# Two-layer FoX and NSA decoder on one core: the second layer's attention units reordered, its filling work spread, and its first output tiles begun apart

## The chip, the cores and the metric

The kernel runs on one core of a Trainium2 chip. The metric is device time in microseconds (us) of one execution. Three timed runs of the kernel before gave a median of 1553.28 us (1551.80 to 1553.96).

A core has five engines that run side by side, each in its own fixed order: TensorE (PE, matrix products and transposes), VectorE (DVE), ScalarE (ACT), GpSimd (POOL), and SyncE (SP), from whose queue this kernel issues all its DMA transfers. An engine waits at the head of its queue until what that instruction needs is there; everything behind it waits too. PEld is PE's loading of the stationary operand, which overlaps with its products.

## The reference, cut to what matters

```python
def reference(x, norm_g, fox..., nsa..., final_g):        # x: 1024 tokens x 1024, f32
    for i in range(2):
        h = rmsnorm(x, norm_g[i])
        y = fox_mixer(h, ...) if i % 2 == 0 else nsa_mixer(h, ...)
        x = x + y
    return rmsnorm(x, final_g)

def nsa_mixer(h, ...):                    # 16 heads of 64, 4 groups of 4 heads share k and v
    q, kc, vc, ks, vs, kw, vw, gate, z = split(h @ w_in)
    o_c = attention over 63 compressed blocks             # before the stage of this case
    o_s = softmax(q ks^T, only 8 chosen blocks of 64 keys) vs       # branch 0, "chosen"
    o_w = softmax(q kw^T, only the last 512 keys) vw                # branch 1, "window"
    o = g0 * o_c + g1 * o_s + g2 * o_w
    return (o * silu(z)) @ w_out
```

The change touches the stage that computes `o_s` and `o_w` for all heads, the projection `z` that is computed beside it, and the last product with `w_out`, the residual and the final norm. All matrix products are made of three products of split operands (a high part and a remainder), which keeps float32 accuracy.

## The kernel before, in words

**Layer 0** (FoX attention) and the projections and the compressed branch of layer 1 take the first 982 us and stay as they are.

**Layer 1's attention** (L1351) works on "supers": one head `h` and one half `s` of the tokens (s=1: tokens 512 to 1023, s=0: 0 to 511), in the order s=1, s=0 for each head, 32 in all. A super has eight *units* (`unit`, L1235), one for each branch `y` and each query tile `qi` of 128 tokens. A unit has: the score product on PE into a PSUM tile of two banks from `psS1`, of which there are two (L1256); on DVE the mask and the row minimum, from PSUM to the SBUF tile `P_n` (L1263); on ACT the exponential (L1266). A chosen unit (y=0) leaves `P_n` in a buffer of its own. A window unit (y=1) uses one of four `Pw` buffers, and POOL makes two half-width copies in `hl_n` from it (L1269 and L1270, three buffers), which a DMA transposes into `hT_n` (L1272). Then the *steps* (L1313) of the super follow: transposes of the chosen scores on PE (L1288), their split copies on ACT and DVE (`split_t`, L150 and L151), and the products with v for both branches on PE (L1296 to L1298); transposes of the first blocks need all four chosen units of the super. `finish` (L1323) scales the sums (`u_n` on DVE, `ot_n` on POOL), and after every second head `close` (L1336) transposes, multiplies with silu(z) (L1347) and writes to `oF` in DRAM (L1348).

The units of the next super are laid between the steps of the one before (`run_attn`, L180). In `units` (L1279) the order is: s=1 first the four chosen, then the four window units; s=0 first window, then chosen. Over the supers this gives eight window units in a row, then eight chosen ones.

**The filler** (L1184) is other work that is laid between the main work by `merge` (L208): both sides yield costs (written by hand, in ns of PE work), and the filler goes on while its sum is under 0.33 times that of the main side. It consists of the silu(z) projections of layer 1, two heads at a time (`nsa_zs`, L1167, with 24 products of 512 columns for each half, a yield of 650 behind each three), and of `load_wout` (L521), which loads `w_out` from DRAM in two halves and splits it: four DMAs, then eight copies on ACT (L530) and eight subtractions on DVE (L531) with a yield of 200 after every two. W_out goes into the memory of `hT`, so a half can only be loaded after the last projection of that half of the tokens. The projection of pair p waits until pair p-2 is done, since `z` has four buffers; pairs 6 and 7 are done half by half together.

**The output** (`out_layer`, L673, called for layer 1 at L1361): for each of eight tiles of 128 tokens, in the order 4, 5, 6, 7, 0, 1, 2, 3, the columns of `oF` are loaded (`of`, L692, a buffer of the pool `wp` that is open during the whole program), split by ACT and DVE (L693, L694), and multiplied with W_out in 48 products of 512 columns (L133 to L135) into two PSUM banks; then residual, norm and store. Tile 4 is done in two steps, of rows 0 to 3 and 4 to 7 of the eight blocks of 128 rows (block p belongs to heads 2p and 2p+1).

**What sets the order.** Each engine's order is planned before the run: the order of the program text is the priority, and an instruction is placed earlier where its engine would be free and its data and buffers are there. Pools are opened and released in the text; the pool `fo` of the output (gB, the residual tiles `xr`, the norm tiles) is opened after the pool `at` of the attention is released, and takes its memory:

```python
at.release()
kv[0].release()
fo = tc.alloc_tile_pool(name="fo", bufs=1, reuse_waits="tile")
```

## Time and profile before

| | |
|---|---|
| median of three timed runs | 1553.28 us |
| the profiled execution, its time | 1553.53 us |
| its span (first to last instruction) | 1551.7 us |
| layer 1's attention, from its first scores to its last sums | about 982 to 1453 us |
| output of layer 1, to the end | about 1453 to 1552 us |
| PE busy, share of the span | 1434.4 us, 92% |
| DVE busy | 1063.7 us, 69% |
| ACT busy | 803.3 us, 52% |
| POOL busy | 556.5 us, 36% |

A row of the page or of a view names the engine, the line of the kernel and the operation with its tiles (out<-in). A group's row gives the count, the busy time, the mean duration in ns, and the idle time of the engine just before it with what ended that. A row of the waits gives the engine and line that waited, what it waited for, the sum in us, the number of waits and the longest. "SPq" rows are the issue of DMAs. A busy PE is not PE at its peak, as products are pipelined and their ends are modelled.

### The profile page before, as it was taken

To read this page: it belongs to the slowest core of one execution; us is meant where nothing else is said; L and a number is where in the kernel's file an instruction comes from. 1 tells how busy PE (TensorE), PEld (TensorE's weight loads), DVE (VectorE), ACT (ScalarE), POOL (GpSimd) and SP (SyncE) were. 2 spreads that over 40 slices of the span, in tenths; PEclk is the share of its full clock that TensorE was granted. 3 is DMA by queue.
4 is the path that set the end of the run, shared out by engine and by line. 5 is a ranking of instruction groups with operands and counts; after the bars stand their busy time and mean duration, and the time that the engine had idled before them with its cause. 6 is when DMAs were issued, how large, how long until landed. Compare 5 with 4: busy or idle time off the path is not lost.

```text
span 1551.7 us, 29460 instructions
## 1 busy us (share of the span) xinstructions
PE 1434.4 (92%) x10488; PEld 1188.4 (77%) x10488; DVE 1063.7 (69%) x2756; ACT 803.3 (52%) x2025; POOL 556.5 (36%) x604
## 2 busy tenths in 40 slices
PE   5999999999999787999999979899898998888898
PEld 4888888888787666878888768687787877667686
DVE  6586878778787755457364687787686777678433
ACT  5364646545555643233133655566565666567321
POOL 1232323222233500043241342557647657345300
PEclk9999999999999889999999999999999999899899
DMA  7796767867878756343345586757756856674642
GB/s 263 223 183 146 163 155 156 172 160 149 178 156 174 166 104 231 95 133 96 126 134 176 149 202 179 206 123 151 168 122 143 195 118 137 151 167 113 161 138 95
DMA packets 405763, 242.72 MB, mean 156 GB/s; under 512 B 332464, under 2 KB 353840, under 8 KB 405360
## 3 DMA queue, kind: packets, MB, share of 16 engines
q1 hardware_dynamic: 405616, 240.84, 63.5%
q8 instruction: 83, 1.36, 0.4%
q14 instruction: 64, 0.52, 0.1%
HBM read 120.96 MB, written 44.11 MB: 106 GB/s over the span
## 4 chain that ended last, share of the span: by engine, by line
PE 61%; DVE 16%; ACT 6%; DMA 6%; POOL 6%; issue 4%; SPq 1%; POOLq 0%; DVEq 0%; ACTq 0%
PE S_n L1256 4%; DVE P_n L1263 3%; PE y L133 3%; PE y L135 3%; PE y L134 3%; POOL hl_n L1270 3%; PE ptp_n L1288 2%; PE v L133 2%; PE v L135 2%; PE v L134 2%; PE S L579 2%; PE S L580 2%; PE q L133 2%; PE O L613 2%; PE k L133 2%
## 5 line engine op out<-in xcount | busy, mean ns | idle before, releaser
L1266 ACT ACTIVATE P_n<-P_n,m_n 128x640 f32<-128x640 f32 (+7 forms) x256 | 187.0, 731 | 74.6 <-DVE m_n L1265 37.3
L1256 PE MATMUL S_n<-nk,nq 128*128 128x320 f32 (+5 forms) x768 | 189.0, 356 | 19.4 <-DVE m_n L1263 18.6
L597 ACT ACTIVATE P<-P,m 128x512 f32<-128x512 f32 (+1 forms) x192 | 116.9, 610 | 133.2 <-DVE m L588 132.3
L568 POOL TENSOR_TENSOR Bd<-B,tri 128x128 f32<-128x128 f32 x128 | 62.3, 501 | 245.3 <-DVE m L588 228.5
L1263 DVE CUSTOM_DVE_ANT_0 P_n<-S_n,wmask 128x128 f32<-128x128 f32 (+1 forms) x192 | 113.5, 598 | 53.4 <-POOL hl_n L1270 37.7
L1256 PEld LDWEIGHTS S_n<-nk,nq 128*128 128x128 f32 x768 | 125.2, 194 | 32.3 <-DVE m_n L1263 23.3
L1270 POOL TENSOR_TENSOR hl_n<-P_n,hl_n 128x640 f16<-128x640 f32 (+4 forms) x128 | 141.5, 1109 | 7.5
L599 DVE SCALAR_TENSOR_TENSOR hl<-P,hl 128x512 f16<-128x512 f32 (+1 forms) x192 | 124.1, 664 | 21.8 <-ACT hl L598 20.7
L150 ACT ACTIVATE pth_n<-ptp_n 128x512 f16<-128x512 f32 (+1 forms) x160 | 86.6, 546 | 76.1 <-PE ptp_n L1288 75.4
L1288 PE MATMUL ptp_n<-ident,P_n 128*128 128x128 f32 x576 | 98.2, 292 | 19.3 <-DVE ptl_n L151 10.3
L151 DVE SCALAR_TENSOR_TENSOR ptl_n<-ptp_n,pth_n 128x512 f16<-128x512 f32 (+1 forms) x160 | 100.5, 634 | 20.8 <-ACT pth_n L150 20.1
L1269 POOL CAST hl_n<-P_n 128x640 f16<-128x640 f32 (+4 forms) x128 | 74.1, 584 | 98.7 <-ACT P_n L1266 78.4
L133 PE MATMUL y<-wo,ohi 128*128 128x512 f32 x240 | 96.8, 403 | 8.0 <-ACT ohi L693 8.0
L1288 PEld LDWEIGHTS ptp_n<-ident,P_n 128*128 128x128 f32 x576 | 71.3, 149 | 33.1 <-DVE ptl_n L151 11.9
L134 PE MATMUL y<-wo,ohi 128*128 128x512 f32 x240 | 96.0, 400 | 0.0
L135 PE MATMUL y<-wo,olo 128*128 128x512 f32 x240 | 94.9, 398 | 0.9 <-DVE olo L694 0.9
L598 ACT ACTIVATE hl<-P 128x512 f16<-128x512 f32 (+1 forms) x192 | 92.5, 513 | 4.3 <-DMA pT<-hl 2.8
L1296 PE MATMUL O_n<-nv,pth_n 128*128 128x64 f16 x576 | 76.1, 199 | 3.7 <-ACT pth_n L150 3.7
L579 PE MATMUL S<-KH,Q 128*128 128x512 f32 (+1 forms) x192 | 68.8, 372 | 10.6 <-DVE m L588 10.4
L1297 PE MATMUL O_n<-nv,pth_n 128*128 128x64 f16 x576 | 74.9, 197 | 0.0
L1298 PE MATMUL O_n<-nv,ptl_n 128*128 128x64 f16 x576 | 72.2, 197 | 0.0
L1296 PEld LDWEIGHTS <-pth_n 128*128 128x128 f16 x576 | 53.8, 101 | 21.4 <-ACT pth_n L150 9.1
(384 smaller groups left out, 4517.0 us busy)
## 6 DMA issues: line engine op xcount, KB each, us to landing
nq<-qD SPq DMA_DIRECT2D x64, 256.0 KB
B<-cD SPq DMA_DIRECT2D x16, 512.0 KB
wo<-wD SPq DMA_DIRECT2D x16, 512.0 KB
nq<-qD SPq DMA_DIRECT2D x64, 128.0 KB
of<-oF SPq DMA_DIRECT2D x12, 512.0 KB
x<-in_x_dram SPq DMA_DIRECT2D x8, 512.0 KB
wst_k<-in_fox_w_dram SPq DMA_DIRECT2D x8, 512.0 KB
wst_v<-in_fox_w_dram SPq DMA_DIRECT2D x8, 512.0 KB
```

Of the source, the lines that this page charges most:

```text
L133: T.matmul(ps, wh, mh, start=first, stop=False, **kw)
L134: T.matmul(ps, wh, ml, start=False, stop=False, **kw)
L135: T.matmul(ps, wl, mh, start=False, stop=last, **kw)
L151: V.scalar_tensor_tensor(lo[:, 0:n], pt[:, 0:n], scale, h, OP.mult, OP.subtract)
L597: A.activation(L[:, 0:n], L[:, 0:n], AF.Exp, bias=init, scale=-1.0, accum_out=self.lr[:, col + c:col + c + 1])
L599: V.scalar_tensor_tensor(lo[:, cs], L[:, 0:n], UP, hi[:, cs], OP.mult, OP.subtract)
L1256: T.matmul(ps[:, b, 0:w], self.q[x][:, qi * P:(qi + 1) * P], k[:, k0 + b * w:k0 + b * w + w], start=(x == 0), stop=(x == 1))
L1263: V.tensor_tensor_reduce(dst, src, mk, 1.0, 3e38, OP.add, OP.min, m)
L1266: A.activation(L, L, AF.Exp, bias=m, scale=-1.0, accum_out=self.l[:, y, qi:qi + 1])
L1270: G.tensor_tensor(hl[:, n:2 * n], L, hl[:, 0:n], OP.subtract)
L1288: T.transpose(pt[:, (x + i) * P:(x + i + 1) * P], L[:, kb * P - k0:(kb + 1) * P - k0], ident)
L1296: T.matmul(o, hi, v[:, 0:64], start=first, stop=False)
```

## The change

Seven edits, all but the last in layer 1's attention and its filler, in the order of the diff:

1. `merge` gets `cap`: a filler that was held up may be behind its share by at most `cap` (1400 in the call for layer 1), and what is beyond that is forgotten.
2. `load_wout` yields 2000 after the four DMAs of a half, and 400 before each copy, for layer 1 alone.
3. `nsa_zs`: pair 6 is projected like the pairs before it; only pair 7 is done half by half, each followed by a half of W_out.
4. There are five `Pw` buffers in place of four, and one `u` buffer in place of two.
5. `units` alternates for both halves: qi 0 chosen, qi 0 window, qi 1 chosen, and so on.
6. The filler's share is 0.36 in place of 0.33.
7. `out_layer` takes `early`, for layer 1 tiles 4 and 5. Their products with blocks 0 to 3 and 4 to 6 are written ahead of the loop of tiles, into the two double banks of the scores; block 7 follows in the loop. For all tiles of layer 1, `of` comes from the pool `fo` with three buffers in place of `wp` with one, and the residual is loaded after the products are issued.

```diff
-    def merge(main, fill, ratio, off=0.0, until=None, rebase=False):
+    def merge(main, fill, ratio, off=0.0, until=None, rebase=False, cap=1e9):
...
             paid += c
+            base = min(base, done + cap - ratio * (paid + off))
             while done < base + ratio * (paid + off):
...
             dma(f(lo[:, k, :]), wD[i][r * P:(r + 1) * P, :])
+        if i:
+            yield 2000
         for k in range(4):
             for c in range(2):
+                if i:
+                    yield 400
                 cs = slice(c * 512, c * 512 + 512)
...
-    def out_layer(ow, w, src, res, g, after, name):
+    def out_layer(ow, w, src, res, g, after, name, early=()):
+
         gB = ow.tile([P, D], F32, name=f"gB{name}")
...
+        def tiles(t):
+            if not early:
+                return out_tiles(f"{name}_{t}")
+            of = ow.tile([P, KC, P], F32, tag="of", bufs=3, name=f"of{name}_{t}")
+            return of, *out_parts(f"{name}_{t}")
+
+        def products(t, tile, ys, ks):
+            of, oh, ol = tile
+            c = slice(ks[0], ks[-1] + 1)
+            dma(of[:, c, :], src[:, t * P:(t + 1) * P].rearrange("(k p) t -> p k t", p=P)[:, c, :])
+            A.copy(oh[:, c, :], of[:, c, :])
+            V.tensor_tensor(ol[:, c, :], of[:, c, :], f(oh[:, c, :]), OP.subtract)
+            for half, ts in enumerate(cs):
+                if len(ys) <= half:
+                    ys.append(ps_a(f"y{name}_{t}_{half}"))
+                for k in ks:
+                    wh, wl = w[k // 4]
+                    mm3(ys[half], oh[:, k, :], ol[:, k, :], wh[:, k % 4, ts], wl[:, k % 4, ts], k == 0, k == KC - 1)
+
+        begun = {}
+        for t in early:
+            ps = ps_s2(f"y{name}_{t}")
+            begun[t] = tiles(t), [ps[:, half, :] for half in range(2)]
+            for ks in (range(0, 4), range(4, 7)):
+                products(t, *begun[t], ks)
         for t in (4, 5, 6, 7, 0, 1, 2, 3):
...
+            if t in begun:
+                tile, ys = begun.pop(t)
+                steps = (range(7, 8),)
+            elif not ys:
+                tile = tiles(t)
             for ks in steps:
...
+                products(t, tile, ys, ks)
+            dma(xt, res[tk, :])
...
     def nsa_zs():
-        for p in range(6):
+        for p in range(7):
             wo_copy(1, p)
             if p >= 2:
                 yield lambda p=p: ("done", p - 2) in ready
             yield from nsa_z(p, next_w(("z", p)))
-        for p in (6, 7):
-            wo_copy(1, p)
-        yield lambda: ("done", 4) in ready
-        ws = [next_w(("z", 6)), next_w(("z", 7))]
+        wo_copy(1, 7)
+        yield lambda: ("done", 5) in ready
+        w = next_w(("z", 7))
         for half in (1, 0):
-            for p in (6, 7):
-                yield from nsa_z(p, ws[p - 6], (half,))
-                if half == 1:
-                    yield lambda: ("done", 5) in ready
+            yield from nsa_z(7, w, (half,))
             yield from load_wout(h1, 1, half)
...
-                L = at.tile([P, 640], F32, tag="Pw", bufs=4, name=f"P_{nm}")[:, 0:n]
+                L = at.tile([P, 640], F32, tag="Pw", bufs=5, name=f"P_{nm}")[:, 0:n]
...
-            return [self.unit(y, qi) for y in ((0, 1) if self.s else (1, 0)) for qi in range(4)]
+            return [self.unit(y, qi) for qi in range(4) for y in range(2)]
...
-            u = at.tile([P, 4, 2, 64], F32, tag="u", bufs=2, name=f"u_{self.name}")
+            u = at.tile([P, 4, 2, 64], F32, tag="u", bufs=1, name=f"u_{self.name}")
...
-    merge(run_attn([NsaSuper(h, s) for h in range(H) for s in (1, 0)], 0.8, 3), filler, 0.33)
+    merge(run_attn([NsaSuper(h, s) for h in range(H) for s in (1, 0)], 0.8, 3), filler, 0.36, cap=1400)
...
-    out_layer(fo, ready["wout"], oF, x1, a["final_g"], after1, 1)
+    out_layer(fo, ready["wout"], oF, x1, a["final_g"], after1, 1, (4, 5))
```

## The prediction, made before the result was known

> **What bounds the kernel now.** I read the page first, then busy time by stretches, then the waits of layer 1's attention, and last the order of single instructions at its two odd places. By stretches (us of PE, PEld, DVE, ACT, POOL busy; then PE's granted clock, DMA share, GB/s):

> ```profile
> 982.00:1453.00 471.00, 422.46 (x4932) 359.41 (x4931) 347.48 (x949) 295.40 (x706) 274.95 (x320) 0.95 0.66 146
> ...
> 1110.00:1120.00 10.00, 7.04 (x59) 6.45 (x60) 5.37 (x15) 3.47 (x9) 7.92 (x11) 0.66 0.68 136
> 1340.00:1350.00 10.00, 3.53 (x36) 2.84 (x34) 3.89 (x7) 4.60 (x9) 0.00 (x0) 0.71 0.71 234
> 1380.00:1390.00 10.00, 5.65 (x94) 4.15 (x91) 4.88 (x16) 4.47 (x12) 5.71 (x9) 0.93 0.98 201
> 1400.00:1453.00 53.00, 46.27 (x611) 39.44 (x610) 38.77 (x113) 33.07 (x82) 32.20 (x39) 0.87 0.53 116
> 1453.00:1552.00 99.00, 88.75 (x384) 72.09 (x382) 34.89 (x58) 22.50 (x49) 2.52 (x3) 0.97 0.42 136
> 300.00:400.00 100.00, 99.65 (x637) 81.42 (x636) 81.99 (x242) 56.27 (x144) 26.37 (x32) 1.00 0.72 155
> ```

> In the 471 us of attention no engine is full: PE stands idle for 471 - 422.5 = 48.5 us, DVE is busy for 347.5/471 = 74%, and layer 0's attention (last row) shows that DVE can reach 82%. Engines wait for each other in turn. Who waits for whom between 980 and 1480 us (sum, times, longest):

> ```profile
> POOL hl_n L1269 <- ACT P_n L1266: 78.4, 18, 16.1
> ACT pth_n L150 <- PE ptp_n L1288: 75.4, 64, 5.0
> ...
> DVE P_n L1263 <- POOL hl_n L1270: 37.7, 36, 3.3
> ...
> PE S_n L1256 <- DVE m_n L1263: 18.6, 18, 2.6
> ...
> ACT wo L530 <- DMA wo<-wD: 11.7, 4, 4.9
> ```

> The first and the third row belong together: POOL starves for up to 16.1 us at a stretch, and at other times DVE stands still for POOL, 36 times, with all that is queued behind it (the split copies `ptl_n`, for which PE's products wait). That is the order of eight window and eight chosen units. Where it is worst (1110 to 1120 us) PE's idle time also brings its clock down to 0.66.

> [...]

> **The change, part by part.** *Alternating units, fifth `Pw` buffer.* Costs of the units' instructions (first count, busy us, mean ns, idle before; then count, shortest/median/longest ns, first and last start):

> ```profile
> L1263 DVE CUSTOM_DVE_ANT_0 P_n<-S_n,wmask 128x128 f32<-128x128 f32 (+1 forms) x192 | 113.5, 598 | 53.4 <-POOL hl_n L1270 37.7
> L1270 POOL TENSOR_TENSOR hl_n<-P_n,hl_n 128x640 f16<-128x640 f32 (+4 forms) x128 | 141.5, 1109 | 7.5
> L1269 POOL CAST hl_n<-P_n 128x640 f16<-128x640 f32 (+4 forms) x128 | 74.1, 584 | 98.7 <-ACT P_n L1266 78.4
> ...
> L1263 DVE CUSTOM_DVE_ANT_0 P_n<-S_n,bias 128x1024 f32<-128x1024 f32 x16 | 19.5, 1220 | 0.3 <-PE S_n L1256 0.2
> L1266 ACT ACTIVATE P_n<-P_n,m_n 128x1024 f32<-128x1024 f32 x16 | 18.3, 1147 | 0.4 <-DVE m_n L1263 0.3
> ...
> L1270 POOL TENSOR_TENSOR hl_n<-P_n,hl_n x128: 425/1314/1919, 996.5 to 1445.7; 128x640 f16<-128x640 f32 x64, 128x128 f16<-128x128 f32 x16, 128x256 f16<-128x256 f32 x16, 128x384 f16<-128x384 f32 x16
> ...
> L1331 DVE TENSOR_TENSOR u_n<-O_n,l_n x32: 677/685/693, 1010.1 to 1452.7; 128x512 f32<-128x512 f32 x32
> ...
> L1263 DVE CUSTOM_DVE_ANT_0 P_n<-S_n,wmask x192: 280/618/826, 992.3 to 1446.2; 128x640 f32<-128x640 f32 x64, 128x128 f32<-128x128 f32 x32, 128x256 f32<-128x256 f32 x32, 128x384 f32<-128x384 f32 x32
> ```

> POOL needs (141.5 + 74.1)/16 = 13.5 us for a head's eight window units, all in one run; in the other half of the head it has next to nothing. Over the whole head POOL has 275/16 = 17.2 us of work and DVE 347.5/16 = 21.7, against a mean period of 471/16 = 29.4. Alternating gives POOL one window unit (1.7 us on average) for every two units of DVE, so neither waits long. The amount removed lies between nothing (the wait moves elsewhere) and the whole 37.7 us. PE's idle time that it can be taken from is 48.5 less the W_out stalls below, some 37. I take half of that, **-18**, since DVE in-order waits are partly covered by filler on PE. A stage of 471 - 31 = 440 us (all parts) has DVE at 79%, below layer 0's 82%, so DVE would not forbid it. One `u` buffer instead of two costs nothing: `u_n` comes once in (1452.7 - 1010.1)/31 = 14.3 us, and POOL reads it at once when it isn't backed up.

> [...]

> *W_out's copies.* ACT and DVE had them queued ahead of the attention's own work before the data was there:

> ```profile
> 1343.72 1.14 ACT L530 CAST wo<-wo 128x512 fp32r<-128x512 f32 x2 [4.88 <-DMA wo<-wD]
> ...
> L530 ACT CAST wo<-wo x16: 607/617/618, 1343.7 to 1396.0; 128x512 fp32r<-128x512 f32 x16
> ...
> 1341.28 7.25 DMA wo<-wD
> ```

> Two stretches of 10 us lost 6.5 and 4.4 us of PE there. The 2000 behind the DMAs are 2000/0.36 = 5.6 us of main work, which at the stage's pace (by the yields in the code a head has 17 us of it: 7.1 of scores, 9.5 of steps, 0.4 of closing; it takes 29) is more than 7.25 us. So the wait of 11.7 us falls; between 0 and 11.7, I take **-10**. The 16 copies (0.62 us ACT, 0.69 DVE each) stay. As the waits of 6.0 us per half count as filler, pair 7 and W_out need (2 x 5.2 + 2 x 6.0)/0.36 = 62 us of main work behind head 11; four heads have about 68, so W_out just ends with the last head.

> *Pair 6, cap and 0.36.* Before, pairs 6 and 7 came in a block at 1326 to 1341 us, and the last stretch (1400 to 1453) had no filler at all: PE idle 6.7 us. Spread out, it fills some of that: 0 to -6.7, I take **-3**.

> *The first output tiles.* Here I expect a loss. Issue of DMAs on SP at the end of both layers, and tile 4's copies on ACT:

> ```profile
> 559.47 14.11 SPq L600 DMA_TRANSPOSE pT<-hl  x6
> 584.88 0.33 SPq L638 DMA_DIRECT2D oF<-z  x1
> 586.93 0.36 SPq L692 DMA_DIRECT2D of<-oF  x1
> 590.56 0.33 SPq L638 DMA_DIRECT2D oF<-z  x1
> 591.00 0.38 SPq L675 DMA_DIRECT2D gB<-in_norm_g_dram  x1
> ...
> L692 SPq DMA_DIRECT2D of<-oF x9: 370/377/381, 1265.9 to 1514.7; - x9
> ...
> 1453.53 0.33 SPq L1348 DMA_DIRECT2D oF<-no  x1
> 1455.54 0.38 SPq L692 DMA_DIRECT2D of<-oF  x1
> 1457.14 0.32 SPq L1348 DMA_DIRECT2D oF<-no  x1
> 1457.55 0.38 SPq L675 DMA_DIRECT2D gB<-in_final_g_dram  x1
> 1457.99 0.44 SPq L696 DMA_DIRECT2D xr<-x  x1
> ...
> 1458.35 0.62 ACT L693 CAST ohi<-of 128x512 fp32r<-128x512 f32 x1 [7.34 <-DMA of<-oF]
> ```

> gB needs only an input, yet in both layers it is issued 0.4 us behind the attention's last write to `oF`; in layer 0 SP had nothing to do between 573.6 and 584.9 and did not issue it. I read this as: a pool that takes over a released pool's memory opens, in the planned order, only behind the last user of the old one. `of` from `wp`, which is always open, was issued at 1265.9, and tile 4's first 24 products were run beside the last head (from 1449.3). The change moves `of` into `fo`: then it comes behind the last write and behind gB, and no early product is early. Before, the pieces on the path were:

> ```profile
> 1449.31 0.31 PE y L133
> ...
> 1457.99 5.95 DMA xr<-x
> 1464.03 0.70 DVE xr L704
> ...
> 1467.23 0.80 PE y L133
> ...
> 1544.96 0.24 PE y L135
> ```

> From 1467.23 to 1545.20 PE ran 336 products without a stop, 0.232 us each. After, with the last write again at 1457.14: `of` is issued where xr was, at 1457.99, and lands after 2.8 us (the 256 KB from 1455.54 to 1458.35, alone) to 5.95 us (xr, behind gB). I take 4.4, between the two as it is half of xr's size: 1462.4, ACT's copy 0.62, PE starts at 1463.0, and has all 384 products to do: 89.1 us, and 0.7 for tile 6, whose operands wait for tile 4's buffers: 1552.8 against 1545.2, **+7.6** (6.0 to 9.2). Residuals now loaded after the products no longer hold ACT, which is why it isn't 11.

> The sum: -18 - 10 - 3 + 7.6 = -23.4. The profiled execution took 1553.5 us (1.8 around its span), 0.25 over the median, so this goes for the median too: **1530 us**; with each part at its ends but alternating at 8 to 30, 1515 to 1545.

> **The rivals.** *The early tiles are early.* If `of` opens with the last use of the tiles it lies on (masks, last read until 1446.8), 60 more products fit into PE's time up to 1467.2. Of those 20.4 us PE used 11.1 for 48 products and an estimated 3.7 for the last head (by the yields 2.8 of steps and 0.9 of closes), so 5 are free: -5 in place of +7.6, **1517**. For it: `of` of tile 4 did get hoisted before. Against: gB in both layers.

> *Alternating wins nothing*: the wait moves from DVE to PE's transposes, the stage is DVE's. Then -10 - 3 + 7.6: **1548**. For it: heads 14 and 15 have no filler and are no quicker than others; against: POOL's gaps of 16 us.

> *Alternating costs.* For s=1 the last chosen score moves from fourth to seventh place of eight, and the transposes of the next steps need it: DVE 1.22 + 0.08, ACT 1.15 + 0.19 = 2.64 us. Before, four window units of 0.82 us on DVE lay between; now one, so 1.8 us are open per head, 16 x 1.8 = 29: 1530 + 29 = **1559**. It decides from 23.4/16 = 1.5 us a head. Against: for s=0 it is the other way round (before, nothing lay between), and PE has the next super's scores and filler to run meanwhile.

> **How the numbers follow.** Forecast 0.60, early tiles early 0.13, nothing won 0.14, alternating costs 0.13. The range 1508 to 1556 leaves out most of the costly case and the lower part of the early one, about 0.2. A change under 0.2%, 3.1 us, can't be told from none: faster than 1550.2 are nearly all of the forecast and the early case and two thirds of "nothing won", 0.80; same 0.07; slower 0.13.

> **What would show it.** Right: DVE's wait for POOL (L1270) below 15 us; ACT's wait for W_out's DMA below 3; POOL's longest starvation below 6 us; first `y` product only behind the last `O_n` product, its `of` issued behind gB. Wrong: `of` issued before the last `oF` write (first rival); PE's transposes or scores waiting for ACT's `P_n` or DVE's `m_n` (18.6 us now) longer by more than DVE's wait for POOL falls (third); or first to last `u_n`, 442.6 us now, not under 430 (second).

## The result, and the profile after

The changed kernel takes **1529.26 us** (median of 4 runs, 1522.62 to 1530.55) against 1552.54 us before (median of 4, 1549.75 to 1553.96). The ratio is 0.9843, with a 95% interval of 0.9816 to 0.9870. The forecast was 1530. Executions of one kernel differ by some us, and the longer ones mostly had the lower mean granted clock (the kernel before on one chip: 1549.70 us at 0.972, 1559.88 at 0.963). The profiled execution took 1529.59 us with a span of 1527.8, which is 23.9 us less than the span before.

The total hides two sums of opposite sign. The last write to `oF` is issued at 1422.07 in place of 1457.14, so the attention ends 35.1 us earlier. From there to the end of the span it was 94.6 us and is now 105.7, so the output takes 11.2 us more. Lines are those of the changed kernel: the scores are L1275, the mask and minimum L1282, the window units' copies on POOL L1288 and L1289, the last sums `u_n` L1350, the write to `oF` L1367, W_out's copies L536 and L537, `of` L696, its copies L697 and L698.

Busy time of the changed kernel by stretches (PE, PEld, DVE, ACT, POOL, then PE's granted clock, DMA share, GB/s): the attention, and the start of the output.

```profile
982.00:1418.00 436.00, 406.90 (x4936) 348.66 (x4934) 352.74 (x957) 296.29 (x706) 284.54 (x322) 0.98 0.73 160
1425.00:1430.00 5.00, 0.83 (x2) 0.61 (x3) 0.85 (x2) 1.13 (x2) 0.00 (x0) 0.50 1.10 294
1430.00:1435.00 5.00, 5.00 (x15) 4.01 (x15) 1.97 (x5) 1.63 (x4) 0.00 (x0) 0.62 1.10 339
```

The first row answers to the 471 us row of before. PE's idle time is 436 - 406.9 = 29.1 us in place of 48.5, and PE's busy time for as many products is 406.9 in place of 422.46, which fits the clock, granted at 0.98 in place of 0.95 (worked out below for the order alone). DVE is now busy for 81%.

The waits of the changed kernel between 980 and 1480 us (sum, times, longest), those of the prediction's list:

```profile
POOL hl_n L1288 <- ACT P_n L1285: 107.8, 58, 6.3
...
PE S_n L1275 <- DVE m_n L1282: 8.3, 13, 1.4
...
ACT wo L536 <- DMA wo<-wD: 7.2, 4, 2.6
DVE P_n L1282 <- POOL hl_n L1289: 6.8, 7, 1.1
```

DVE's wait for POOL fell from 37.7 to 6.8 us. POOL still starves, for more in sum than before, but for 6.3 us at the longest in place of 16.1, in 58 short pieces. ACT's wait for W_out's data fell only from 11.7 to 7.2. PE's wait for the scores' buffers, which DVE frees, fell from 18.6 to 8.3.

SP's issue of DMAs at the end of the changed kernel, and then the chain of waits there (start, duration):

```profile
1422.07 0.33 SPq L1367 DMA_DIRECT2D oF<-no  x1
1422.48 0.38 SPq L682 DMA_DIRECT2D gB<-in_final_g_dram  x1
1422.92 2.96 SPq L696 DMA_DIRECT2D of<-oF  x5
```

```profile
1422.92 5.56 DMA of<-oF
1428.50 0.63 ACT ohi L697
1429.17 0.80 PE y L133
1429.97 0.43 PE y L134
```

gB comes 0.4 us behind the last write to `oF`, and `of` right behind gB: no tile is early. The last `O_n` product ended at 1417.15 and the first `y` product starts at 1429.17. The first products take 0.43 us each in place of 0.23, at a clock of 0.50 to 0.62 (the rows from 1425 to 1435 above); the full clock is back after 1433.8. The clock was already halved at 1416.72, behind a stop of PE of 2.3 us in the last head, and stayed so through two more stops of 1.6 and 9.3 us.

### The profile page after: what moved, and what is told of

Read it like the earlier page. It is cut to its first block, busy times and chain, and to the rows that moved or that the text cites. A ratio compares the mean times of both kernels' runs of the same rounds, so it can differ in the third digit from the quotient of the medians.

```text
span 1527.8 us, 29541 instructions
## 1 busy us (share of the span) xinstructions
PE 1421.9 (93%) x10488; PEld 1179.8 (77%) x10488; DVE 1066.2 (70%) x2759; ACT 805.1 (53%) x2028; POOL 565.1 (37%) x604
## 4 chain that ended last, share of the span: by engine, by line
PE 63%; DVE 16%; ACT 8%; DMA 6%; issue 4%; POOL 1%; SPq 1%; POOLq 0%; DVEq 0%; ACTq 0%
PE S_n L1275 5%; PE y L133 3%; PE y L135 3%; PE y L134 3%; PE ptp_n L1307 3%; ACT P_n L1285 2%; DVE P_n L1282 2%; PE v L133 2%; PE v L135 2%; PE v L134 2%; DVE hl L605 2%; PE S L585 2%; ACT P L603 2%; PE k L133 2%; PE k L134 2%
## 5 line engine op out<-in xcount | busy, mean ns | idle before, releaser
L1275 PE MATMUL S_n<-nk,nq 128*128 128x320 f32 (+5 forms) x768 | 180.0, 350 | 8.6 <-DVE m_n L1282 8.3
L1289 POOL TENSOR_TENSOR hl_n<-P_n,hl_n 128x640 f16<-128x640 f32 (+4 forms) x128 | 145.0, 1133 | 9.8
L1275 PEld LDWEIGHTS S_n<-nk,nq 128*128 128x128 f32 x768 | 125.2, 193 | 20.9 <-DVE m_n L1282 10.8
L605 DVE SCALAR_TENSOR_TENSOR hl<-P,hl 128x512 f16<-128x512 f32 (+1 forms) x192 | 124.6, 667 | 20.5 <-ACT hl L604 19.5
L1282 DVE CUSTOM_DVE_ANT_0 P_n<-S_n,wmask 128x640 f32<-128x640 f32 (+2 forms) x192 | 113.4, 595 | 25.7 <-PE S_n L1275 16.0
L1288 POOL CAST hl_n<-P_n 128x640 f16<-128x640 f32 (+4 forms) x128 | 77.0, 601 | 122.1 <-ACT P_n L1285 107.8
L150 ACT ACTIVATE pth_n<-ptp_n 128x512 f16<-128x512 f32 (+1 forms) x160 | 85.9, 547 | 49.9 <-PE ptp_n L1307 48.8
L133 PE MATMUL y<-wo,ohi 128*128 128x512 f32 x240 | 97.5, 406 | 15.4 <-ACT ohi L697 13.9
L1307 PE MATMUL ptp_n<-ident,P_n 128*128 128x128 f32 x576 | 92.4, 281 | 9.4 <-DVE ptl_n L151 4.3
L135 PE MATMUL y<-wo,olo 128*128 128x512 f32 x240 | 95.9, 402 | 0.8 <-DVE olo L698 0.8
L604 ACT ACTIVATE hl<-P 128x512 f16<-128x512 f32 (+1 forms) x192 | 92.5, 513 | 4.5 <-DMA pT<-hl 3.1
L1307 PEld LDWEIGHTS ptp_n<-ident,P_n 128*128 128x128 f32 x576 | 66.9, 143 | 20.8 <-DVE ptl_n L151 9.5
L585 PE MATMUL S<-KH,Q 128*128 128x512 f32 (+1 forms) x192 | 68.1, 368 | 11.3 <-DVE m L594 10.9
L1315 PE MATMUL O_n<-nv,pth_n 128*128 128x64 f16 x576 | 72.0, 196 | 6.5 <-ACT pth_n L150 5.5
L727 DVE TENSOR_TENSOR xr<-y,xr 128x512 f32<-128x512 f32 x32 | 21.5, 689 | 73.5 <-PE y L135 65.6
L1315 PEld LDWEIGHTS <-pth_n 128*128 128x128 f16 x576 | 52.2, 98 | 25.3 <-ACT pth_n L150 11.1
L1316 PE MATMUL O_n<-nv,pth_n 128*128 128x64 f16 x576 | 71.0, 194 | 0.0
```

What stands on the lines that cost most here:

```text
L133: T.matmul(ps, wh, mh, start=first, stop=False, **kw)
L135: T.matmul(ps, wl, mh, start=False, stop=last, **kw)
L605: V.scalar_tensor_tensor(lo[:, cs], L[:, 0:n], UP, hi[:, cs], OP.mult, OP.subtract)
L1275: T.matmul(ps[:, b, 0:w], self.q[x][:, qi * P:(qi + 1) * P], k[:, k0 + b * w:k0 + b * w + w], start=(x == 0), stop=(x == 1))
L1282: V.tensor_tensor_reduce(dst, src, mk, 1.0, 3e38, OP.add, OP.min, m)
L1289: G.tensor_tensor(hl[:, n:2 * n], L, hl[:, 0:n], OP.subtract)
```

## The experiments

Twelve kernels were run, each beside runs of the kernel before on the same chip. The ratio to those is the better measure between kernels of different chips. "Attention" and "output" come from each kernel's profiled execution: the end of the last `O_n` product, and the time from there to the end of the last `y` product. The profiled execution can lie some us off its kernel's median: 5.8 us above it in x1, 4.6 above in x8, 3.0 below in x3.

| kernel | median us | ratio (95%) | attention ends | output us |
|---|---|---|---|---|
| before | 1552.54 | 1 | 1452.7 | 92.5 |
| after | 1529.26 | 0.9843 (0.9816 to 0.9870) | 1417.2 | 103.8 |
| x1 after, old output | 1518.30 | 0.9783 (0.9770 to 0.9796) | 1422.0 | 93.8 |
| x2 before, new output | 1561.57 | 1.0063 (1.0050 to 1.0075) | 1451.9 | 101.6 |
| x3 after, early pieces from `wp` | 1514.87 | 0.9755 (0.9741 to 0.9768) | 1413.9 | 89.4 |
| x4 before, order and buffers | 1519.80 | 0.9792 (0.9775 to 0.9809) | 1419.8 | 93.9 |
| x5 before, W_out spread | 1552.55 | 0.9985 (0.9969 to 1.0002) | 1452.1 | 92.4 |
| x6 before, filler spread | 1550.92 | 0.9970 (0.9956 to 0.9983) | 1449.0 | 94.6 |
| x7 before, order alone | 1518.50 | 0.9767 (0.9742 to 0.9792) | 1417.8 | 92.8 |
| x8 before, buffers alone | 1540.60 | 0.9906 (0.9882 to 0.9929) | 1441.8 | 95.1 |
| x9 before, runs of four | 1531.75 | 0.9860 (0.9838 to 0.9882) | 1434.6 | 91.1 |
| x10 = x3, W_out's subtractions on POOL | 1520.74 | 0.9791 (0.9769 to 0.9814) | 1424.8 | 88.0 |
| x11 = x3, chosen units ahead | 1518.66 | 0.9779 (0.9758 to 0.9801) | 1421.0 | 89.4 |
| x12 order alone, early pieces from `wp` | 1517.85 | 0.9787 (0.9765 to 0.9810) | 1420.6 | 88.1 |

### The output edit, undone and alone (x1, x2)

x1 is the changed kernel with `out_layer` of before; x2 is the kernel before with `out_layer` of the change and nothing else.

```diff
-    out_layer(fo, ready["wout"], oF, x1, a["final_g"], after1, 1, (4, 5))
+    out_layer(fo, ready["wout"], oF, x1, a["final_g"], after1, 1)        # x1, with the old function
```

> The changed kernel with the output function of before: only the seventh edit is undone. My theory (the output edit costs what the tail grew by in the two traces, 105.7 - 94.6 = 11 us, since no product comes early): 1529 - 11 = 1518 us, 1514 to 1522, with 24 y products beside the last head and the last write to oF where the changed kernel has it (1422). Rival (the output edit wins, and the longer tail comes from the attention that ends earlier): 1533 or more. Second rival (the output edit makes no difference): 1529.

> The kernel before with the seventh edit alone (early, of from the pool fo, residuals behind the products). My theory: the tail behind the last write grows from 94.6 to about 105 us, the attention stays: 1552.5 + 11 = 1563 us, 1559 to 1566. By the term of my prediction: 1560. Rival (early products win): 1547.

Measured: 1518.3 and 1561.57. Both fall to the theory and against the rivals. Undoing the edit wins 0.0060 of the ratio, 9.3 us (11.0 between the medians); adding it alone costs 0.0063, 9.8 us (7.8 to 11.6). (In x1 the last write to `oF` came at 1427.78, not at the 1422 that was expected.) In x2 the same order on SP and the same stop are seen with the old attention (SP's issue, and PE's first `y` product with the idle time ahead of it):

```profile
1452.65 3.93 SPq L1365 DMA_DIRECT2D oF<-no  x2
1456.67 0.38 SPq L676 DMA_DIRECT2D gB<-in_final_g_dram  x1
1457.11 2.73 SPq L690 DMA_DIRECT2D of<-oF  x5
```

```profile
1463.40 0.80 PE L133 MATMUL y<-wo,ohi 128*128 128x512 f32 x1 [9.30 <-ACT ohi L691]
```

### Early products that are early (x3, x12)

```diff
-            of = ow.tile([P, KC, P], F32, tag="of", bufs=3, name=f"of{name}_{t}")
+            of = None if t in early else ow.tile([P, KC, P], F32, tag="of", bufs=3, name=f"of{name}_{t}")
...
-            of, oh, ol = tile
+            of, oh, ol = (wp.tile([P, KC, P], F32, tag="wst", bufs=1, name=f"of{name}_{t}_{ks[0]}") if t in early else tile[0], *tile[1:])
```

> The changed kernel, but the early tiles 4 and 5 take each piece of oF from the buffer of the pool that is always open (one buffer, a new tile for each piece), so their operands can be there before the attention ends. My theory (the loss is the pool's late opening and nothing else): PE goes from the last O_n product into y products without a stop; the 84 early products (19.5 us) cover the last write and the load of block 7, so the 7 us of stop go, and the stop at tile 6 with them: 1529 - 11 to 1529 - 17, 1512 to 1518 us. Rival (copies of the early pieces hold ACT and DVE up in the last heads, or the stop only moves to block 7 or to the residuals): 1525 to 1530.

Measured: 1514.87, inside the theory's range, and 14 us under the changed kernel. It is the lowest of all medians here. SP issues pieces of `of` ahead of the last write, while gB, in the pool `fo` still, comes 0.85 us behind that write, right after the piece of `of` that waited for that write; PE's rows by 5 us show no stop behind the last `O_n` product (1413.9):

```profile
1407.68 0.53 SPq L696 DMA_DIRECT2D of<-oF  x1
...
1413.72 0.33 SPq L1367 DMA_DIRECT2D oF<-no  x1
1416.12 0.33 SPq L696 DMA_DIRECT2D of<-oF  x1
1419.11 0.32 SPq L1367 DMA_DIRECT2D oF<-no  x1
1419.54 0.37 SPq L696 DMA_DIRECT2D of<-oF  x1
1419.96 0.45 SPq L682 DMA_DIRECT2D gB<-in_final_g_dram  x1
```

```profile
1415.00:1420.00 5.00, 5.00 (x20) 4.06 (x19) 1.56 (x2) 0.30 (x1) 1.77 (x2) 0.72 0.11 37
1420.00:1425.00 5.00, 5.00 (x24) 4.14 (x23) 0.29 (x1) 0.30 (x1) 0.00 (x0) 1.00 0.95 264
```

So the first rival of the prediction was right about what early tiles would be worth, and wrong that the change makes them early. Against the old output (x1, on the same chip) the gain is 0.0028 of the ratio, 4.3 us, as the output's 93.8 and 89.4 us say.

x12 takes the kernel before with the order of units alone (x7) and this output:

> The kernel before with two edits: the alternating order (fifth edit alone) and the output with early products from the always open pool; four Pw and two u buffers, W_out's copies, pair 6, cap and share as before. If the two effects add and the other edits win nothing beside them: 1518.5 - 4 (the early-product kernel beside the changed kernel with the old output, 1518.3 to 1514.9) = 1514 to 1516 us. If the other edits (W_out spread, filler spread) still win something once products run beside the last head: 1518 to 1525. If they only cost DVE and ACT time at a bad place: under 1511.

Measured: 1517.85, ratio 0.9787. This lies between the 1514 to 1516 of the first case and the 1518 to 1525 of the second, and the intervals of x12, x7 and x3 overlap at their edges. The output is shorter by 4.7 us than in x7, but the attention ended 2.8 us later in the profiled execution. The trace speaks against copies that hold up the last heads: from 982 us to its end of the attention PE stood idle for 27.0 us in x12 and 26.6 in x7. The rest is busy time, with the clock at half for 20.5 and 17.1 us.

### The order and the buffers (x4, x7, x8)

x7 is one line, x8 two sizes, x4 both:

```diff
-            return [self.unit(y, qi) for y in ((0, 1) if self.s else (1, 0)) for qi in range(4)]
+            return [self.unit(y, qi) for qi in range(4) for y in range(2)]                       # x7, x4
...
-  tag="Pw", bufs=4     tag="u", bufs=2
+  tag="Pw", bufs=5     tag="u", bufs=1                                                           # x8, x4
```

> The kernel before with the fourth and fifth edits alone: alternating units, five Pw buffers, one u buffer. My theory: most of the attention's gain is here, 18 to 22 us: 1531 to 1535 us, DVE's wait for POOL (37.7 us) under 12. Rival (alternating wins nothing by itself, W_out and the filler win it all): 1550 to 1554. Third (it costs, the last chosen score being later): 1560 or more.

> The kernel before with the fifth edit alone: alternating units, with four Pw buffers and two u buffers as before. If the order is what wins (POOL gets one window unit for every two of DVE): 1519 to 1524, DVE's wait for POOL between 5 and 15 us. Rival (the fifth buffer takes the wait away, the order alone only half of it): 1530 to 1540, DVE's wait for POOL over 20.

> The kernel before with the fourth edit alone: five Pw buffers, one u buffer, the order of units as before. If the order is what wins: 1548 to 1553, a fifth buffer shortens each run of eight window units by one wait at most, 16 times 0.3 us. Rival (the buffer wins): 1535 to 1545.

Measured: 1519.8, 1518.5 and 1540.6. The order wins 36 us by itself (0.0233 of 1554.6), far more than the 18 of the forecast and the 18 to 22 expected of x4. The buffers win 14.6 us by themselves, where 1548 to 1553 was expected: that the fifth buffer shortens a run by one short wait at most was wrong. Beside the order they win nothing that can be told (x4 against x7), so at least part of what the two take away is the same stall. DVE's wait for POOL fell further than expected, to 0.4 us in x7 and 14.1 in x8. The row of x7 for the attention, then who PE waits for there, before and in x7:

```profile
982.00:1418.00 436.00, 409.45 (x4937) 350.99 (x4937) 347.71 (x956) 296.29 (x706) 278.80 (x321) 0.98 0.75 160
```

```profile
PE ptp_n L1288 <- DVE ptl_n L151: 10.3, 12, 3.0
PE ptn_n L1345 <- DVE ptl_n L151: 4.7, 1, 4.7
PE ptp_n L1288 <- DVE m_n L1265: 4.4, 6, 1.4
```

```profile
PE O_n L1296 <- ACT pth_n L150: 9.4, 7, 3.8
PE S_n L1256 <- DVE m_n L1263: 5.0, 11, 1.4
PE ptp_n L1288 <- DVE ptl_n L151: 3.4, 6, 1.2
...
PE O_n L1298 <- DVE ptl_n L151: 1.8, 3, 0.6
```

Of the 35 us that the stage is shorter in x7, 48.5 - (436 - 409.45) = 22.0 are PE's idle time, and 422.46 - 409.45 = 13.0 are the same work done in less busy time, at a granted clock of 0.98 in place of 0.95. The idle part shows in PE's own waits: with the 18.6 us of scores, PE stood for 38.0 us behind DVE before (18.6 + 10.3 + 4.7 + 4.4), and 10.2 in x7 (5.0 + 3.4 + 1.8). These are 27.8 us less, but its wait for `pth_n` on ACT grew from 3.7 to 9.4. (Both hold stops at W_out's copies: the single wait of 4.7 before, and two of 3.3 and 3.8 for ACT in x7.)

The part of the clock can be worked out too. In the traces of before and after the granted clock was either full or half (1.00 or 0.50), and in this stage it changed only at steps of 3.41 us. It was at half for 51.2 us of the stage before and for 17.1 in x7. PE was busy in 40.2 and 13.8 us of these, and at full clock that work would take an estimated half of the time (the output's products in the changed kernel took 0.43 us at half and 0.23 at full clock): 20.1 - 6.9 = 13.2 us, which meets the 13.0. A step need not be wholly idle for it: PE was busy for 1.31 us of the one ahead of the halved ones here. These are five steps in a row of the kernel before, full, full, half, half, full:

```profile
1105.27:1108.68 3.41, 1.96 (x22) 1.32 (x20) 3.10 (x9) 1.87 (x7) 3.41 (x4) 1.00 0.76 143
1108.68:1112.10 3.42, 1.31 (x12) 0.82 (x8) 0.36 (x1) 0.48 (x1) 3.42 (x3) 1.00 0.49 125
1112.10:1115.51 3.41, 2.55 (x20) 2.25 (x21) 2.38 (x8) 1.19 (x3) 3.25 (x5) 0.50 0.66 125
1115.51:1118.92 3.41, 3.41 (x24) 3.22 (x23) 1.72 (x6) 2.28 (x6) 1.57 (x4) 0.50 0.95 133
1118.92:1122.34 3.42, 3.42 (x55) 2.78 (x55) 1.80 (x6) 1.58 (x5) 2.89 (x4) 1.00 1.00 285
```

In the attention of before and after the clock fell to half behind 13 such steps, nine and four. PE was busy for 0 to 53% of 11 of them, and for 62% and 65% of the other two. Behind every step with less than 50% the next was at half, and the full clock came back only behind steps with 89% or more. So in these two traces stops that add up to 1.8 us in a step were enough for half the clock in the next.

### Runs of four (x9)

```diff
-            return [self.unit(y, qi) for y in ((0, 1) if self.s else (1, 0)) for qi in range(4)]
+            return [self.unit(y, qi) for y in range(2) for qi in range(4)]
```

> The kernel before with one other edit: every super first its four chosen, then its four window units (before, the s=0 supers had the windows first, so eight window units came in a row; four now, and there are four Pw buffers). If the stall is a run of windows longer than the buffers, runs of four are as good as alternating alone (1518.5): 1517 to 1525, DVE's wait for POOL under 6. If fine alternation is needed, POOL being idle for four chosen units and late for four window ones: 1530 to 1545. Third rival of the prediction (late last chosen score costs): here the last chosen score is at place four of eight for both halves, so this would be faster than alternating: 1510 or less.

Measured: 1531.75, the second case (1530 to 1545) by its time, but not by its reason: DVE's wait for POOL is gone here too (1.9 us), as the first case had it. So runs no longer than the buffers take DVE's wait away, and that order is worth 21.8 us; the other 14 that alternating wins come from elsewhere. PE's two longest waits in x9 show one place:

```profile
PE O_n L1296 <- DMA hT_n<-hl_n: 8.8, 8, 3.2
PE S_n L1256 <- DVE m_n L1263: 8.5, 6, 4.2
```

We read the first as four window units at the end of every super that come late to POOL, so that their transposing DMAs and the window products are late; x7 has 2.6 us in 2 such waits. No run tests this reading. PE's busy time is 417.56 us here at a clock of 0.96, against 409.45 at 0.98 in x7, which is another 8. The expectation from the third rival of the prediction (1510 or less, with the last chosen score at place four of eight) did not come true.

### W_out's copies and the filler (x5, x6)

x5 is the kernel before with the yields of 2000 and 400 in `load_wout`; x6 has the cap, pair 6 like the others and the share 0.36.

> The kernel before with the second edit alone (2000 behind the DMAs of each half of W_out, 400 ahead of each copy). By my prediction's term: 10 us less (0 to 11.7), 1542. Theory now, after the run with alternating units alone won 32 us by itself and the one with everything but the output edit 34: the wait of ACT for the DMA falls as forecast, but the time is worth at most 2 us, 1550 to 1553, since what PE does not get there is set by DVE, which has the 16 subtractions to do in any case. Third: slower by 3 or more, as W_out ends later than the last head.

> The kernel before with the first, third and sixth edits alone (cap, pair 6 like the ones before it, share 0.36). By my prediction's term: 3 us less (0 to 6.7), 1549. Rival: nothing, 1551 to 1553. Third: slower, because W_out's first half comes no earlier and the second half is pushed behind the last head: 1555 or more.

Measured: 1552.55 and 1550.92. x5's gain of 2.3 us can't be told from none (the interval holds 1.0). x6 wins 4.7 us (2.6 to 6.8). Both together beside the new order and buffers win nothing that can be told: x1 against x4, 0.9783 and 0.9792, with overlapping intervals.

But x5 does not say what ACT's wait is worth, since it hardly took the wait away: 10.4 us are left of 11.7. Its first half's copies start from 1343.7 to 1351.8, as before (1343.7 to 1351.1); only the second half's are spread. In x6, without the yields, the wait was 6.6.

```profile
ACT wo L534 <- DMA wo<-wD: 10.4, 6, 5.8
```

The wait does stop PE. The two longest stops of PE in x7's attention, 3.3 and 3.8 us, end with a `pth_n` that ACT made only behind copies that had waited for W_out. This is the first (ACT, then PE):

```profile
1315.15 1.14 ACT L530 CAST wo<-wo 128x512 fp32r<-128x512 f32 x2 [6.82 <-DMA wo<-wD]
1316.19 1.08 ACT L150 ACTIVATE pth_n<-ptp_n 128x512 f16<-128x512 f32 x2
```

```profile
1316.84 0.24 PE L1296 MATMUL O_n<-nv,pth_n 128*128 128x64 f16 x1 [3.26 <-ACT pth_n L150]
```

Yet where the wait did fall, PE's idle time did not. ACT waits 11.3 us in x12 and 3.1 in x3, both with the new order and early pieces. In the 30 us from the first DMA of each half PE stood idle for 11.4 and 11.8 us in all. (Other work fills these stretches too, and the clock of the second was higher in x3, so a gain by the clock is not excluded.) These are x12, then x3:

```profile
1311.60:1341.60 30.00, 25.26 (x277) 21.22 (x276) 23.09 (x58) 20.25 (x46) 11.04 (x14) 0.94 0.56 149
1349.80:1379.80 30.00, 23.31 (x255) 19.86 (x253) 24.13 (x63) 20.04 (x48) 14.30 (x16) 0.80 0.63 148
```

```profile
1325.20:1355.20 30.00, 24.53 (x302) 21.20 (x301) 27.04 (x67) 22.62 (x54) 16.95 (x20) 0.94 0.79 183
1375.40:1405.40 30.00, 23.66 (x351) 20.07 (x351) 27.76 (x74) 25.58 (x62) 17.86 (x20) 1.00 0.73 181
```

### Two attempts to go further (x10, x11)

```diff
-                (V if i else G).tensor_tensor(lo[:, k, cs], f(lo[:, k, cs]), f(hi[:, k, cs]), OP.subtract)
+                G.tensor_tensor(lo[:, k, cs], f(lo[:, k, cs]), f(hi[:, k, cs]), OP.subtract)      # x10
...
-            return [self.unit(y, qi) for qi in range(4) for y in range(2)]
+            return [self.unit(y, qi) for y, qi in ((0, 0), (0, 1), (1, 0), (0, 2), (1, 1), (0, 3), (1, 2), (1, 3))]   # x11
```

> The kernel with early products from the always open pool (1514.9 before), and W_out's 16 subtractions on POOL in place of DVE. If DVE, busy for 27 of the 30 us from 1330 to 1360, is what keeps PE from its products while W_out is split (PE idle 12 us from 1330 to 1400): 3 to 6 us less, 1509 to 1512. Rival (POOL stands in order behind W_out's data, and its window units come late): 1516 to 1522.

> The kernel with early products from the always open pool (1514.9 before), with the units in the order chosen 0, chosen 1, window 0, chosen 2, window 1, chosen 3, window 2, window 3: the last chosen score at place six in place of seven, POOL still with at most two window units in a row within a super. If the late last chosen score still costs (third rival of the prediction, 1.2 us a head at the most): 1500 to 1510. If it costs nothing, since PE has other work: 1512 to 1518.

Measured: 1520.74 and 1518.66; by the ratios 5.6 us and 3.7 us above x3. x10 went the rival's way: from 1330 to 1360 DVE is relieved to 21.6 us of 30, POOL is busy for 24.0, and PE gets 23.4 in place of the 24.6 that it had in x3:

```profile
1330.00:1360.00 30.00, 23.42 (x288) 20.75 (x286) 21.59 (x64) 23.48 (x56) 23.98 (x26) 0.89 0.72 162
```

PE now waits 6.0 us for `ot_n` from POOL (3 times, 5.0 the longest), a wait that x3 does not have. So moving the load from DVE to POOL does not help PE there; what DVE's load alone costs PE is not shown, as POOL came in its way. x11's interval overlaps x3's at the edge: no gain from earlier chosen scores. The 7.1 us by which its profiled attention is longer are no stops: PE stood idle for 27.2 us there and 29.0 in x3, and the clock was at half for 17.1 and 3.4 us.

## Why the prediction was right, and where it was not

**The total** (1530 against 1529.26) is right, but that it came out so close is luck: alternating won twice what was put for it, and the 13 us put for W_out and the filler could not be told from nothing beside it. The likeliest case's range of 1515 to 1545 is not the sum of its parts' ends either; these give 1511 to 1554.

**Alternating, -18: right mechanism in the main, half its size.** x7 measured -36. The step that failed is "I take half of that, since DVE in-order waits are partly covered by filler on PE". Two things were left out. PE's time behind DVE could have been read directly, 38 us of it, and 27.8 of these went (5.7 came back behind ACT); and the term counted idle time alone, while 13 us came from products that ran at a higher granted clock. The prediction quoted the row with the clock at 0.66 and gave it no price. Nor did it see that part of the gain has little to do with DVE's wait for POOL: x9 took that wait away too and won 22.

**The fifth buffer** was folded into the same term. Alone it wins 14.6 us, beside the order nothing.

**W_out's copies, -10: wrong.** Alone -2.3, not to be told from none. The first step that failed is "So the wait of 11.7 us falls": it fell to 10.4 in x5 and to 7.2 in the changed kernel, not below 3. There the first copy stands at 1332.27, 5.2 us behind the first DMA (issued at 1327.06), although the 2000 was worked out to outlast 7.25 us. A filler that was held up is behind its share and runs through such yields at once; the cap lets it owe 1400 of those 2000. x5, without the cap, fits this, as its first half's copies are not spread at all; no run changes the cap alone. The second step took nearly all of ACT's wait for PE's loss: in x3 the wait is 3.1 us, and PE's idle time about the copies no shorter than in x12 with 11.3.

**Pair 6, cap and share, -3:** -4.7 alone, within its bounds; beside the other edits it can't be told.

**The first output tiles, +7.6: right sign and mechanism, somewhat too small.** 9.3 to 9.8 us by the runs, 11.2 in the profiled execution. There the first product starts 7.1 us behind the last write, not 5.9, since `of` took 5.56 us to land, not 4.4 (within the bounds 2.8 to 5.95). The 384 products then take 91.8 us (1429.17 to 1520.93), not 89.8: the stop ahead of tile 6, at 1464.8, is 1.4 us in place of 0.7, and the low clock of the first eleven costs some 2.2, while the others run a little quicker than the 0.232 that was put. This clock was the forgotten term again: the wait ahead of the products was priced, the clock that they run at was not.

The first products ran at half speed for 4.6 us (1429.17 to 1433.8): one whole step of 3.41 us and the rest of the one in which they began. By the trace that cost 11 x 0.2 = 2.2 us. It did not take a step without products: PE was busy for 1.09 of the 3.41 us ahead of 1416.72, where the clock was halved, and in the kernel before for 0.35 to 2.21 us of such steps in the attention.

**The rivals.** The early tiles were not early (gB and `of` behind the last write, in after and x2). "Alternating wins nothing" was refuted by x7, and so was "alternating costs"; x9 and x11, where the chosen scores come earlier, were no faster either.

**The signs that were named.** DVE's wait for POOL below 15: yes, 6.8. First `y` product behind the last `O_n`, with `of` behind gB: yes. First to last `u_n` under 430: yes, 405.0. POOL's longest starvation below 6: just missed, 6.3. ACT's wait for W_out below 3: no, 7.2; the wait was the wrong thing to price, and it did not go.

**DVE beside POOL.** POOL's subtractions hardly grew in the changed kernel: those of 640 columns took 1406 ns in the median before and 1412 after, and the mean of all went from 1109 to 1133. More shows where W_out's subtractions on DVE now lie beside POOL's (groups of after and of before):

```profile
L1289 POOL TENSOR_TENSOR hl_n<-P_n,hl_n 128x640 f16<-128x640 f32 (+4 forms) x128 | 145.0, 1133 | 9.8
...
L537 DVE TENSOR_TENSOR wo<-wo,wo 128x512 fp32r<-128x512 f32 x16 | 14.2, 890 | 2.8 <-ACT wo L536 2.8
```

```profile
L531 DVE TENSOR_TENSOR wo<-wo,wo 128x512 fp32r<-128x512 f32 x16 | 10.4, 689 | 11.9 <-ACT wo L530 11.9
```

That is 16 x 0.2 = 3.2 us more for DVE; spreading them out put them where POOL works. POOL pays as well: seven of its subtractions that ran beside them took 0.3 to 0.55 us more than the median of their shape, 2.9 us in all, nearly all that the group grew by (128 x 24 ns = 3.1).

## What to carry to other kernels

Where an in-order engine hands work to a slower one (DVE's mask of 598 ns in the mean to POOL's two copies of 584 and 1109), look at the order of the units before the number of buffers: here one line that alternated them won 36 us, more than all seven edits together, and the buffers alone 14.6. Price a stall from the waits of the engine that bounds the stage, and add what its clock loses; a wait of another engine (here ACT's for W_out) is not that price. Before a run is taken to price a wait, see in its trace that the wait went: in x5 it had not. A tile that is to be early must come from a pool that is open by then: writing its products ahead of the loop won nothing, and the edit cost 9 us, while its buffer lay in memory that opened behind the attention.

## What was not expected of the hardware

DVE's subtraction of 128x512 for W_out took 0.68 to 0.73 us before, where POOL did next to nothing beside it, and up to 1.87 us beside POOL's work in the changed kernel. The last of them lay wholly beside a POOL subtraction and took 0.69; then it was POOL's, of 128x384, that took 1.47 us, where 0.92 is the median of that shape:

```profile
1408.08 0.69 DVE L537 TENSOR_TENSOR wo<-wo,wo 128x512 fp32r<-128x512 f32 x1
```

```profile
1408.07 1.47 POOL L1289 TENSOR_TENSOR hl_n<-P_n,hl_n 128x384 f16<-128x384 f32 x1
```
